# A hybrid diffusion backbone: the first block's modulation quarters between its products, later loads behind its weights, two pieces per mix, GpSimd's low parts in the mLSTM

## The chip, the cores and the metric

One core of a Trainium2 chip runs the whole network in one program. The metric is the time of one execution on the device in microseconds (us); lower is better. Five engines work side by side, each through its own list of instructions: TensorE (PE; its weight loads are shown as PEld), VectorE (DVE), ScalarE (ACT), GpSimd (POOL) and SyncE (SP), which here issues the transfers from memory.

## What is computed

Four layers over 256 context and 256 latent tokens of width 1024, in float32. Each layer has a token mixer (chunked MLP, RG-LRU, mLSTM, chunked MLP) and a convolutional FFN; each is preceded by a norm whose scale and shift come from a projection of the conditioning vectors.

```python
for l in range(DEPTH):
    sh1, sc1, g1, sh2, sc2, g2 = split(silu(c) @ mod_w[l] + mod_b[l])     # latent
    csh1, csc1, cg1, ...       = split(silu(c_ctx) @ mod_w[l] + mod_b[l]) # context
    hl = rms_norm(xl, norm1_g[l]) * (1 + sc1) + sh1                       # hc likewise
    ol, oc = mixer[l % 3](hl, hc)
    xl = xl + g1 * ol
    xl = xl + g2 * conv_ffn(rms_norm(xl, norm2_g[l]) * (1 + sc2) + sh2)
    # context likewise; nothing for it after the last layer
return rms_norm(xl, final_norm_g)

def chunk_mlp(h, w_in, b_in, v_g, v_b, w_s, b_s, w_out):
    u, v = split(gelu(h @ w_in + b_in))            # 2048 each
    v = layer_norm(v, v_g, v_b)
    s = einsum('gpq,bnqgc->bnpgc', w_s, v) + b_s   # mixes the 128 tokens of a chunk
    return (u * s) @ w_out

def mlstm_mixer(h):
    q, k, v, o, g = split(h @ w_in)                # g: input and forget gates
    # cumulative sums of log(sigmoid(forget)), running maxima, decayed scores, both directions
    return (sigmoid(o) * rms_norm(hf + hb) * norm_g) @ w_out
```

## The kernel before, in words

**Layout and products.** Activations lie feature-major: 8 tiles of 128 features (k = 0 to 7), 512 tokens along the free axis, 256 of them context and 256 latent. A weight comes as a tile of 128x1024 floats (0.5 MB) by a transfer of SP (`wsplit`, line 206, three buffers `wr`). It is split into a high part `wh` by ScalarE (L214) and the rest, the low part `wl`, by one subtraction of GpSimd, or of VectorE for every `lo_mix`-th weight (L216 to L218; `lo_mix` is 4 unless set, four buffers for each part). Activations are split alike. A product is three matmuls on the parts (`mm3`: L223 high by high, L224, L225).

**Modulation.** The weights `mod_w` of the scale and shift projections are worked off in pieces: a load of 0.5 MB into one of three buffers `mw` (`mod_load`, L113), then four matmuls with the conditioning vectors (`mod_mul`, L124; the trace shows eight rows for each piece). After eight pieces the sum is copied to `mrow` (L131), turned into columns by two matmuls (L140), and VectorE adds bias and gain (L153, L156). The pieces fill TensorE's list between other work: `pump(n)` adds a credit of n and takes a piece for each whole one. The tuple `PR` (L46) holds the credits by place; its second number is the credit per mix of the first chunk MLP, 1.7. `need` does what is still missing before a norm. There are 176 pieces in all; loads run up to three ahead.

**First block** (`first`, from L1045). The first layer's scale and shift are needed at once, so they come from a copy of their weights in four quarters (`mod_w0`), each giving the columns of two k. The squares of x are summed and the inverse root means brought to PSUM as rows over all partitions (`rp`), then copied to two tiles `rb` by ScalarE. A quarter is four loads (L1070), eight `mod_mul`, `mod_columns`, then `scale_shift` for two k and two streams (L374: nt = x * scale * rb on VectorE; L375: the high part of h on ScalarE; L376: its low part on VectorE), then the products of the first 512 value columns for these two k, and from the second quarter on those of two u tiles.

**Rest of the first chunk MLP.** Three more groups of 512 value columns (each with a load `bv`, L570, used at L575), the products `spatial` of the mixing weights (L602), 16 u tiles, and with a lag of four the 16 mixes (`mix`: L641 mixes the tokens, VectorE and GpSimd multiply and split, then `pump`). The output projection (`out_proj`, weights wo) follows. The FFN begins with a load `cv` (L440).

**mLSTM.** Projection to k by weights that stay (`project_by_stream`), gates from the product with `m_wg`, scans over the tokens on VectorE (`fc` and `mx`, L825 to L828), the rest of k and q, gm's exponential on ScalarE (L849), then the values in two halves (`values`). The readout has a norm and a gate.

**What sets the order.** On SP the order in the first block is that in which the code is written (a manual schedule); elsewhere, and on the other engines throughout, a scheduler sets each engine's list at build time from modelled times. `after(later, earlier)` adds a rule that one instruction is issued after another.

## Time and profile before

| | |
|---|---|
| median of 3 runs | 2141.99 us (2139.78 to 2145.58) |
| the profiled execution | 2143.22 us, its span 2141.1 us |
| granted TensorE clock, mean | 0.975 of full speed |
| transfers | 327.70 MB, mean 153 GB/s |
| PE's share of the chain of waits that ended last | 84% |

The profile comes from one execution. Its span runs from the first to the last instruction; the execution's own time is 2.1 us longer. The page gives each engine's busy time, then the span in 40 slices of 53.5 us. The trace gives each instruction, with what ended the idle time before it on its engine, and busy times and the granted clock for any stretch. Times in the trace are counted from the span's start.

### The profile page before, as it was taken

How to read it: one execution, taken by the hardware profiler on the slowest of the kernel's cores; microseconds unless marked ns; L12 is line 12 of the kernel's file. 1: busy time of each engine (PE TensorE's matmuls, PEld its weight loads, DVE VectorE, ACT ScalarE, POOL GpSimd, SP SyncE). 2: the span in 40 equal slices, each digit the busy share in tenths (PEclk: the TensorE clock that was granted, in tenths of full speed). 3: DMA queues.
4: the chain of work that ended last, by engine and by line, in shares of the span. 5: the costliest groups of instructions: out<-in, count | busy, mean ns of one | idle time of the engine just before them, and what ended most of it. 6: DMA issues, size and time to landing. Idle time of an engine off the chain costs nothing.

```text
span 2141.1 us, 33300 instructions
## 1 busy us (share of the span) xinstructions
PE 2046.9 (96%) x12828; PEld 1746.2 (82%) x12828; DVE 1317.3 (62%) x2816; ACT 895.9 (42%) x1388; POOL 978.3 (46%) x599
## 2 busy tenths in 40 slices
PE   6999999999999999999999999999989999999997
PEld 4787688877778876778777778877889987998997
DVE  4344314766565488957665663626768875847886
ACT  3333222433333146724333332536455555555553
POOL 1334331554444010344444442234358874775784
PEclk9999999999999999989999999999989999998998
DMA  8435533345555435432545453334245655554562
GB/s 333 170 106 186 194 103 114 99 163 171 179 168 169 154 120 187 145 96 63 193 163 187 165 183 94 102 118 151 86 132 184 187 175 165 167 168 131 177 185 90
DMA packets 95425, 327.70 MB, mean 153 GB/s; under 512 B 10529, under 2 KB 12193, under 8 KB 95265
## 3 DMA queue, kind: packets, MB, share of 16 engines
q1 hardware_dynamic: 95264, 325.56, 46.4%
q8 instruction: 101, 1.65, 0.3%
q14 instruction: 60, 0.48, 0.1%
HBM read 324.47 MB, written 1.05 MB: 152 GB/s over the span
## 4 chain that ended last, share of the span: by engine, by line
PE 84%; DVE 8%; ACT 2%; issue 2%; DMA 2%; POOL 1%; SPq 0%; DVEq 0%; ACTq 0%; POOLq 0%
PE ps L223 22%; PE ps L224 21%; PE ps L225 21%; PE ps L124 4%; PE ps L505 3%; PE ps L507 3%; PE ps L506 3%; POOL wl L218 1%; DVE wl L218 1%; PE ps L641 1%; PE ps L932 1%; PE ps L362 1%; DVE nt L374 1%; ACT wh L214 1%; DVE cvo L490 1%
## 5 line engine op out<-in xcount | busy, mean ns | idle before, releaser
L218 POOL TENSOR_TENSOR wl<-wr,wh 128x1024 fp32r<-128x1024 f32 (+2 forms) x329 | 751.8, 2289 | 722.8 <-ACT wh L214 672.6
L214 ACT ACTIVATE wh<-wr 128x1024 fp32r<-128x1024 f32 (+2 forms) x413 | 415.0, 1008 | 741.1 <-PE ps L224 338.2
L490 DVE SCALAR_TENSOR_TENSOR cvo<-ps,cv,cvo 128x189 f32<-128x189 f32 (+2 forms) x1344 | 528.6, 427 | 58.1 <-ACT cvo L479 35.5
L223 PE MATMUL ps<-h,wh 128*128 128x512 f32 (+1 forms) x1256 | 445.0, 365 | 7.4 <-ACT h L375 5.9
L224 PE MATMUL ps<-h,wh 128*128 128x512 f32 (+1 forms) x1256 | 447.9, 359 | 1.8 <-DVE h L376 1.8
L225 PE MATMUL ps<-h,wl 128*128 128x512 f32 (+1 forms) x1256 | 447.2, 359 | 0.0
L223 PEld LDWEIGHTS ps<-h,wh 128*128 128x128 f32 x1256 | 232.3, 189 | 63.6 <-ACT wh L214 9.4
L224 PEld LDWEIGHTS ps<-h,wh 128*128 128x128 f32 x1256 | 238.2, 190 | 36.6 <-DVE h L376 2.6
L225 PEld LDWEIGHTS ps<-h,wl 128*128 128x128 f32 x1256 | 238.1, 190 | 35.7 <-issue 0.2
L218 DVE TENSOR_TENSOR wl<-wr,wh 128x1024 fp32r<-128x1024 f32 (+1 forms) x108 | 138.6, 1284 | 121.8 <-ACT wh L214 120.7
L224 PE MATMUL ps<-hn,wh 128*128 128x256 f32 x608 | 175.5, 289 | 7.0 <-DVE hn L376 6.9
L223 PE MATMUL ps<-hn,wh 128*128 128x256 f32 x608 | 174.9, 288 | 5.8 <-ACT zs L469 3.8
L225 PE MATMUL ps<-hn,wl 128*128 128x256 f32 x608 | 174.7, 288 | 0.0
L505 PE MATMUL ps<-hid,wh 128*128 128x256 f32 (+1 forms) x504 | 156.7, 324 | 8.4 <-ACT hid L234 8.4
L506 PE MATMUL ps<-hid,wh 128*128 128x256 f32 (+1 forms) x504 | 160.2, 322 | 0.9 <-POOL hid L235 0.9
L507 PE MATMUL ps<-hid,wl 128*128 128x256 f32 (+1 forms) x504 | 155.4, 321 | 0.6 <-POOL wl L218 0.6
L481 DVE SCALAR_TENSOR_TENSOR cvo<-ps,cv,cvo 128x255 f32<-128x255 f32 x84 | 40.5, 482 | 169.2 <-ACT cvo L479 169.2
L223 PE MATMUL ps<-prod,wh 128*128 128x256 f32 (+1 forms) x432 | 139.5, 328 | 4.2 <-DVE prod L232 3.1
L224 PE MATMUL ps<-prod,wh 128*128 128x256 f32 (+1 forms) x432 | 139.8, 325 | 1.5 <-POOL prod L235 1.3
L225 PE MATMUL ps<-prod,wl 128*128 128x256 f32 (+1 forms) x432 | 139.6, 325 | 0.6 <-DVE wl L218 0.6
L224 PEld LDWEIGHTS ps<-hn,wh 128*128 128x128 f32 x608 | 119.1, 196 | 8.6 <-DVE hn L376 8.6
L223 PEld LDWEIGHTS ps<-hn,wh 128*128 128x128 f32 x608 | 119.4, 197 | 6.8 <-ACT zs L469 4.6
(241 smaller groups left out, 3579.1 us busy)
## 6 DMA issues: line engine op xcount, KB each, us to landing
mw<-mod_w SPq DMA_DIRECT2D x192, 512.0 KB, 4.7
wr<-w_up SPq DMA_DIRECT2D x168, 512.0 KB, 3.6
wr<-w_dn SPq DMA_DIRECT2D x42, 512.0 KB, 3.7
wr<-cm_wv SPq DMA_DIRECT2D x32, 512.0 KB, 4.1
wr<-cm_wu SPq DMA_DIRECT2D x32, 512.0 KB, 3.6
wr<-cm_wo SPq DMA_DIRECT2D x32, 512.0 KB, 3.7
wr<-w_dn SPq DMA_DIRECT2D x42, 256.0 KB, 2.7
wr<-w_down SPq DMA_DIRECT2D x24, 448.0 KB, 3.4
```

Of the source, the lines that this page charges most:

```text
L124: PE.matmul(mps[0][32 * q:32 * q + 32, :w], ccp[:, k], raw[:, q * w:(q + 1) * w], start=k == 0, stop=k == KT - 1, tile_position=(0, 32 * q ...
L214: S.activation(hi[:, :n], raw[:, :n], AF.Copy)
L218: e.tensor_tensor(lo[:, :n], raw[:, :n], hi[:, :n].bitcast(F32), op=OP.subtract)
L223: PE.matmul(out, lh, rh, start=start, stop=False)
L224: PE.matmul(out, lh, rl, start=False, stop=False)
L225: PE.matmul(out, ll, rh, start=False, stop=stop)
L362: PE.matmul(o, q[:, t * P:(t + 1) * P], ones[:, :1], start=i == t == 0 and q is parts[s][0], stop=q is parts[s][-1], skip_group_check=True)
L481: V.scalar_tensor_tensor(o[:, 1:T], z[:, 0:T - 1], w(3), o[:, 1:T], op0=OP.mult, op1=OP.add)
L490: V.scalar_tensor_tensor(od, zl[:, r0 + dr:r1 + dr, c0 + dc:c1 + dc], w(tap), od, op0=OP.mult, op1=OP.add)
L505: PE.matmul(o, hi[:, sl], rh, start=first, stop=False, skip_group_check=True)
L506: PE.matmul(o, hi[:, sl], rl, start=False, stop=False, skip_group_check=True)
L507: PE.matmul(o, lo[:, sl], rh, start=False, stop=i == FT - 1, skip_group_check=True)
```

## The change

Four things, in the order of the diff:

1. The credit per mix of the first chunk MLP is 2 instead of 1.7.
2. While the first block is written, loads of `mod_w`, of the later `bv` and of `cv` get a rule that they are issued after the block's last weight load (`last_w`).
3. `first` is rearranged. The weights of quarter q+1 (modulation and values) are loaded ahead; quarter q+1's modulation products are written between the value products of k = 2q and those of k = 2q+1, its columns and norm behind the latter. All low parts of weights in the block are VectorE's (`lo_mix` 1). The rows `rp` are read from PSUM by L374, with no copies to `rb`. The `fence` set there is gone.
4. In the mLSTM, after the first products of k, all low parts are GpSimd's (`lo_mix` of a million), until the first half of the values is done.

```diff
@@ -43,7 +43,7 @@
 
 MV = ((1, 0), (2, 4), (3, 5))
 
-PR = (2, 1.7, 0, 2.2, 0, 1.3, 0, 2.2, 0, 2.7, 0, 0, 0)
+PR = (2, 2, 0, 2.2, 0, 1.3, 0, 2.2, 0, 2.7, 0, 0, 0)
 
 KO = (2, 8, 3)
 NHP = 700
@@ -110,10 +110,12 @@
 
     def mod_load(grp, k):
         raw = mwp.tile([P, D], F32, tag="mw", name="mw")
-        SP.dma_start(raw, a["mod_w"][grp[0] * 6 + grp[1] * 2 + grp[2] - 2, k])
+        d = SP.dma_start(raw, a["mod_w"][grp[0] * 6 + grp[1] * 2 + grp[2] - 2, k])
+        if last_w[0] is not None:
+            after(d, last_w[0])
         return raw
 
-    mps = [None]
+    mps, last_w, wdma = [None], [None], [None]
 
     def mod_mul(raw, grp, k):
 
@@ -203,7 +205,7 @@
     lo_mix = [4]
     def wsplit(src, n):
         raw = wraw.tile([P, D], F32, tag="wr", name="wr")
-        SP.dma_start(raw[:, :n], src)
+        wdma[0] = SP.dma_start(raw[:, :n], src)
         return split(raw, n)
 
     def split(raw, n):
@@ -437,7 +439,7 @@
     def ffn(l, streams, npump):
         W = T * len(streams)
         cv = tmp.tile([P, 420], F32, tag="cv", name="cv", bufs=1)
-        SP.dma_start(cv, a["conv"][l])
+        after(SP.dma_start(cv, a["conv"][l]), last_w[0])
         names = [(0, 0), (1, 0), (0, 1), (1, 1)][:STG[3] if len(streams) == 2 else 4]
         Z = {}
         late = ahead[0] is not None
@@ -567,7 +569,9 @@
 
         def evacuate(c, pss):
             bv = tmp.tile([P, 512], F32, tag="cvo", name="bv", bufs=4)
-            SP.dma_start(bv, bass.AP(tensor=a["cm_bv"].tensor, offset=a["cm_bv"][j, c].offset, ap=[[0, P], [1, 512]]))
+            d = SP.dma_start(bv, bass.AP(tensor=a["cm_bv"].tensor, offset=a["cm_bv"][j, c].offset, ap=[[0, P], [1, 512]]))
+            if l == 0:
+                after(d, last_w[0])
             for t in range(ntt):
                 if t % 2 == 0:
                     v[t // 2, c] = big([P, 2, 512], F32, "v")
@@ -796,6 +800,7 @@
         normed(l, 1, [CTX, LAT], h)
         hl = [t[:, :, T:W] for t in h]
         zk = project_by_stream([a["m_wk"][n] for n in range(STG[5])], KT, h, [CTX, LAT], k_outer=True)
+        lo_mix[0] = 10 ** 6
 
         NR = 36
         p = psum()
@@ -974,6 +979,7 @@
                 split_act(prod[i], t, e)
 
         values(0)
+        lo_mix[0] = 4
         gcol = big([P, 4, NR], F32, "gcol")
         pt = psum()
         for t in range(4):
@@ -1052,9 +1058,7 @@
         rsqrt(r, rp[:, :4], 4, 1.0 / D)
         for t in range(4):
             PE.matmul(rp[:, t * P:(t + 1) * P], r[:, t:t + 1].to_broadcast([P, P]), ident, start=True, stop=True)
-        rb = [tmp.tile([P, T], F32, tag=f"acc{s}", name="rb", bufs=1) for s in BOTH]
-        for s in BOTH:
-            S.activation(rb[s], rp[:, s * T:s * T + T], AF.Copy)
+        lo_mix[0] = 1
         pss = [psum() for t in range(4)]
         pu = [psum() for _ in range(2)]
         wu = []
@@ -1063,29 +1067,54 @@
             for k in range(k0, k1):
                 sl = slice(k * P, (k + 1) * P)
                 mm3(pu[n], (wu[n][0][:, sl], wu[n][1][:, sl]), pair(h[k], 0, 2 * T), k == 0, k == KT - 1)
-        for q in range(4):
+        def weights(q):
             grp = (0, 0, q // 2, q % 2)
+            raws = []
             for k in range(0, KT, 2):
                 raw = big([P, 2, 512], F32, "mw0")
                 SP.dma_start(raw.rearrange("p k x -> p (k x)"), a["mod_w0"][q, k // 2])
-                for kk in range(2):
-                    mod_mul(raw[:, kk], grp, k + kk)
+                raws.append(raw)
+            return raws
+
+        def quarter(q, raws):
+            for k in range(KT):
+                mod_mul(raws[k // 2][:, k % 2], (0, 0, q // 2, q % 2), k)
+
+        def norm(q):
             mod_columns(*pend.pop(0))
-            w = wsplit(a["cm_wv"][0, 0, :, q * 1024:q * 1024 + 1024], 1024)
+            for k in (2 * q, 2 * q + 1):
+                for s in BOTH:
+                    scale_shift(0, 1, s, k, rp[:, s * T:s * T + T], h[k][:, :, s * T:s * T + T], [])
+
+        def values(k, w):
+            sl = slice(k % 2 * 512, k % 2 * 512 + 512)
+            for t in range(4):
+                mm3(pss[t], pair(h[k], t * P, t * P + P), (w[0][:, sl], w[1][:, sl]), k == 0, k == KT - 1)
+        def values_w(q):
+            return wsplit(a["cm_wv"][0, 0, :, q * 1024:q * 1024 + 1024], 1024)
+        raws = weights(0)
+        w = values_w(0)
+        quarter(0, raws)
+        norm(0)
+        for q in range(4):
+            if q < 3:
+                nw = values_w(q + 1)
+                nxt = weights(q + 1)
             if q in (1, 2):
                 wu.append(wsplit(a["cm_wu"][0, q - 1], D))
-            for k in (2 * q, 2 * q + 1):
-                norm = []
-                for s in BOTH:
-                    scale_shift(0, 1, s, k, rb[s], h[k][:, :, s * T:s * T + T], norm)
-                sl = slice(k % 2 * 512, k % 2 * 512 + 512)
-                for t in range(4):
-                    mm3(pss[t], pair(h[k], t * P, t * P + P), (w[0][:, sl], w[1][:, sl]), k == 0, k == KT - 1)
+            values(2 * q, w)
+            if q < 3:
+                quarter(q + 1, nxt)
+            values(2 * q + 1, w)
+            if q < 3:
+                norm(q + 1)
             if q > 0:
                 u_tile(0, 0 if q == 1 else 2 * q, 2 * q + 2)
             if q > 1:
                 u_tile(1, 0 if q == 2 else 2 * q, 2 * q + 2)
-        fence[0] = norm[-1]
+            w = nw
+        lo_mix[0] = 4
+        last_w[0] = wdma[0]
         ms.__exit__(None, None, None)
         evacuate(0, pss)
         for i in range(2):
```

The orders below are those of the built programs; line numbers of the change are two to five higher.

VectorE, first block, first two quarters (m: scale and shift columns; nt: x scaled; h: low half of the normed tile; wl: a weight's low part; rb, ps: the root means, in SBUF and in PSUM). Before:

```order
L153 TENSOR_TENSOR m_222<-ps,pc 128x2x2
L156 SCALAR_TENSOR_TENSOR m_219<-m_219,pc 128x2x2
L374 SCALAR_TENSOR_TENSOR nt<-x_82,m_219,rb 128x256 x2
L374 SCALAR_TENSOR_TENSOR nt<-x_83,m_219,rb 128x256 x2
L376 SCALAR_TENSOR_TENSOR h<-nt,m_222,h 128x256 x4
L218 TENSOR_TENSOR wl<-wr,wh 128x1024
```

And with the change:

```order
L220 TENSOR_TENSOR wl<-wr,wh 128x1024
L155 TENSOR_TENSOR m_221<-ps,pc 128x2x2
L155 TENSOR_TENSOR m_224<-ps,pc 128x2x2
L158 SCALAR_TENSOR_TENSOR m_221<-m_221,pc 128x2x2
L376 SCALAR_TENSOR_TENSOR nt<-x_82,m_221,ps 128x256 x2
L376 SCALAR_TENSOR_TENSOR nt<-x_83,m_221,ps 128x256 x2
L378 SCALAR_TENSOR_TENSOR h<-nt,m_224,h 128x256 x4
L220 TENSOR_TENSOR wl<-wr,wh 128x1024
```

The low parts that GpSimd made beside these now stand on VectorE between the norms: two ahead of the first, one behind each of the first two, one inside the third, one ahead of the fourth. On TensorE the second quarter's modulation products stand behind the value products of both first k, not between them; the third's and fourth's stand among the products of the quarter before. On SP two value weights follow the first quarter's four loads, then come the second quarter, a value weight, the third quarter, a u and a value weight, the fourth quarter and the last u weight. Behind these stand the loads that came ahead of the second quarter before: three of `mod_w`, four `bv`, one `cv`.

TensorE, end of the mixes (L641, with the change L645: mixing products; L124, L126: modulation pieces of four; L140, L142: columns; L223 to L227: the products of the output projection). Before:

```order
L124 MATMUL ps<-mw,ccp 32x256 x8
L641 MATMUL ps<-ws,v 128x128 x4
L124 MATMUL ps<-mw,ccp 32x256 x4
L641 MATMUL ps<-ws,v 128x128 x8
L124 MATMUL ps<-mw,ccp 32x256 x12
L140 MATMUL ps<-sel_96,mrow 128x8 x2
L124 MATMUL ps<-mw,ccp 32x256 x4
L641 MATMUL ps<-ws,v 128x128 x4
```

And with the change:

```order
L126 MATMUL ps<-mw,ccp 32x256 x8
L645 MATMUL ps<-ws,v 128x128 x4
L126 MATMUL ps<-mw,ccp 32x256 x4
L645 MATMUL ps<-ws,v 128x128 x5
L142 MATMUL ps<-sel_96,mrow 128x8 x2
L645 MATMUL ps<-ws,v 128x128 x6
L126 MATMUL ps<-mw,ccp 32x256 x4
L645 MATMUL ps<-ws,v 128x128
L225 MATMUL ps<-prod,wh 128x512
```

Of the pieces behind the last projection four now stand among the mixing products, and six follow among the first fifty products of the output projection (behind 5, 20, 24, 26, 45 and 47 of them).

ScalarE, the mLSTM's gates (wh: high part of a weight; km, qm: k and q; gm: the gates). Before:

```order
L841 ACTIVATE km<-ps 128x512 x4
L847 ACTIVATE qm<-ps 128x256
L214 ACTIVATE wh<-wr 128x1024
L847 ACTIVATE qm<-ps 128x256
L849 ACT_TABLE_LOAD
L849 ACTIVATE gm<-gm 36x256
```

And with the change:

```order
L846 ACTIVATE km<-ps 128x512 x4
L852 ACTIVATE qm<-ps 128x256
L854 ACT_TABLE_LOAD
L854 ACTIVATE gm<-gm 36x256
L216 ACTIVATE wh<-wr 128x1024
L852 ACTIVATE qm<-ps 128x256
```

One high part has moved from before gm's exponential to behind it. On VectorE the low part between the scans of mx and the rest of the gates is gone.

## Rows read from the trace of the kernel before

**Rows 1.** The page: busy time by engine, then tenths in 40 slices.

```profile
PE 2046.9 (96%) x12828; PEld 1746.2 (82%) x12828; DVE 1317.3 (62%) x2816; ACT 895.9 (42%) x1388; POOL 978.3 (46%) x599
...
PE   6999999999999999999999999999989999999997
...
PEclk9999999999999999989999999999989999998998
```

**Rows 2.** Timeline, first block: start, length (us), instructions [idle before, releaser].

```profile
29.12 1.95 PE L124 MATMUL ps<-mw,ccp 128*32 128x128 f32 x64
...
32.35 5.89 DVE L374 SCALAR_TENSOR_TENSOR nt<-x,m,rb 128x256 f32<-128x256 f32 x4
...
32.50 5.06 POOL L218 TENSOR_TENSOR wl<-wr,wh 128x1024 fp32r<-128x1024 f32 x2 [12.53 <-ACT wh L214]
...
33.42 0.50 PE L223 MATMUL ps<-h,wh 128*128 128x512 f32 x1 [1.50 <-ACT wh L214]
...
38.69 1.22 PE L225 MATMUL ps<-wh,h 128*128 128x512 f32 x2 [0.25 <-DVE h L376]
...
50.57 1.67 DVE L374 SCALAR_TENSOR_TENSOR nt<-x,m,rb 128x256 f32<-128x256 f32 x4
...
58.38 0.39 PE L223 MATMUL ps<-wh,h 128*128 128x512 f32 x1
...
59.06 0.39 PE L223 MATMUL ps<-wh,h 128*128 128x512 f32 x1
...
77.82 1.98 PE L602 MATMUL ps<-ws,ones 128*128 128x512 f32 x4
```

**Rows 3.** Timeline, end of the mixes, SP's queue and TensorE.

```profile
246.48 0.80 SPq L113 DMA_DIRECT2D mw<-mod_w  x2
...
248.57 18.62 SPq L113 DMA_DIRECT2D mw<-mod_w  x7
...
251.33 0.64 PE L124 MATMUL ps<-mw,ccp 128*32 128x256 f32 x8 [0.27 <-DMA mw<-mod_w]
...
255.94 1.08 PE L124 MATMUL ps<-mw,ccp 128*32 128x256 f32 x8 [3.98 <-DMA mw<-mod_w]
```

**Rows 4.** Windows there: stretch, length, busy PE PEld DVE ACT POOL, PEclk, DMA, GB/s.

```profile
250.00:254.00 4.00, 1.70 (x21) 0.61 (x19) 3.57 (x5) 1.59 (x3) 2.66 (x3) 1.00 0.91 295
254.00:264.00 10.00, 7.49 (x35) 5.20 (x36) 1.68 (x4) 1.28 (x3) 2.00 (x3) 0.50 0.62 220
```

**Rows 5.** Timeline, the mLSTM's gates.

```profile
1383.61 2.41 POOL L218 TENSOR_TENSOR wl<-wr,wh 128x1024 fp32r<-128x1024 f32 x1 [2.43 <-ACT wh L214]
...
1383.98 3.11 DVE L825 TENSOR_TENSOR_SCAN fc<-lf,t 4x512 f32<-4x512 f32 x1
...
1391.54 1.21 DVE L825 TENSOR_TENSOR_SCAN mx<-t,ig 4x512 f32<-4x512 f32 x1
...
1394.26 1.22 DVE L218 TENSOR_TENSOR wl<-wr,wh 128x1024 fp32r<-128x1024 f32 x1
...
1395.53 0.80 PE L224 MATMUL ps<-wl,h 128*128 128x512 f32 x1 [5.50 <-DVE wl L218]
```

**Rows 6.** Windows there, columns as in rows 4.

```profile
1390.00:1395.50 5.50, 0.03 (x1) 0.00 (x0) 5.35 (x7) 0.00 (x0) 0.44 (x2) 0.87 0.00 0
1395.50:1401.00 5.50, 5.47 (x13) 4.32 (x14) 2.88 (x14) 1.86 (x4) 3.51 (x1) 0.51 0.59 192
```

**Rows 7.** Windows of the first 40 us, columns as in rows 4.

```profile
0.00:20.00 20.00, 7.52 (x81) 6.50 (x81) 7.43 (x23) 8.31 (x14) 2.79 (x6) 1.00 0.92 342
20.00:40.00 20.00, 14.95 (x104) 11.04 (x105) 11.63 (x23) 6.90 (x13) 5.06 (x2) 0.80 1.02 399
```

**Rows 8.** Timeline, TensorE: norm of first FFN, of second FFN, mLSTM readout.

```profile
354.55 1.50 PE L124 MATMUL ps<-mw,ccp 128*32 128x256 f32 x24
...
961.55 1.01 PE L223 MATMUL ps<-h,wh 128*128 128x256 f32 x3 [1.19 <-ACT h L375]
...
1522.44 1.06 PE L124 MATMUL ps<-mw,ccp 128*32 128x256 f32 x14
```

## The prediction

> **What bounds the kernel now.** I read the page first: TensorE is busy for 2046.9 of 2141.1 us, and of 40 slices only the first and the last are well below nine tenths; the clock falls below nine tenths in four [rows 1]. What is lost inside the others, windows of a few us show. Work on the other engines costs nothing unless TensorE waits for it. So the change is worth what it takes from TensorE's waits and from the stretches in which its granted clock is at the lower level (1.2 of 2.4 GHz), and that is settled place by place. I went on to the timeline of the first 80 us, of the end of the first mixer's mixes, and of the mLSTM's gates.
>
> First block, second quarter [rows 2]: its modulation products begin at 29.12 and take 1.95, and TensorE goes on with the next tiles at 33.42. Then the four nt take 5.89 us, because two low parts of GpSimd run in the same stretch; the first low half of h reaches TensorE at 38.69. The row of 50.57 is to be read beside that of 32.35: the same four instructions, 1.67 us with GpSimd idle.
>
> End of the mixes [rows 3]: after the last projection the pieces of modulation follow each other faster than their weights land, and one waits 3.98 us. The stretches show the whole price [rows 4]: TensorE idles 4.0 - 1.70 = 2.3 and 10.0 - 7.49 = 2.5 us, and 7.49 busy us at a granted clock of 0.50 lose another 3.7: 8.5.
>
> mLSTM's gates [rows 5, 6]: the second product of the values waits 5.50 us for a low part that stands on VectorE behind the gate scans. Idle 5.5; then 5.47 busy us at 0.51 lose 2.7. Together 8.2.
>
> **The change part by part**, against the profiled execution (2143.2 us; the runs' median is 2142.0, 1.2 below).
>
> *First block.* All six low parts go to VectorE; the later loads (three of mod_w, four bv, cv: 2.8 MB) no longer stand on SP ahead of the second quarter; rb is read from PSUM, which I cost at nothing (bounds 0 and 0.4 for four nt: the rows of nt differ by that much only beside GpSimd). Up to 33.42 I leave the instants as they are: the new order still has quarter 1 behind the products of both first tiles, and its columns with nothing beside them. From there TensorE has 120 products of 512 columns; three take 59.06 - 58.38 = 0.68 [rows 2], so 27.2 us; two quarters of 1.95, 3.9; four pieces (8 rows each; 24 rows are 1.50, so 0.5 each [rows 8]), 2.0; some five gaps of 0.3 where it changes to modulation products, 1.5. The third norm has a low part of VectorE (1.22 [rows 5]) behind its columns and loses some 1.0 to it; the later columns have 12 and 18 products of u beside them, 2.7 and 4.1 us. The sum is 33.4 + 35.6 = 69.0 for the spatial products, which now begin at 77.82. Three pieces fewer are done by then, 1.5: 77.8 - 69.0 - 1.5 = 7.3; I take **7.0** (bounds 3, as in rival 2, and 9, with no wait left). Are the weights there? At 342 and then 399 GB/s [rows 7] 6.8 MB are in at 20 us and 14.8 at 40; the last quarter ends with the 13.4th, in at 37, wanted near 52. On ScalarE quarter 0's mrow now stands behind a second wh, whose weight ends with the 5.5th MB, in at 16 to 17: nothing, at most 1 us.
>
> *More pieces per mix* (1.7 to 2): always two. A piece costs 0.5 wherever TensorE has other work, and the number of all pieces stays. After the last projection there are ten instead of nine, but the order now has four of them among the mixes and six among the first 50 products of the output projection. Measured from the end of the last projection, loads are issued at +1.7 (two, [rows 3]: 246.48) and the second is used at 251.33, 4.9 us on; the next ones land about 1.6 us apart (0.5 MB at the 295 GB/s of [rows 4]). By that the fourth piece, at +7, has its weight at +6; the fifth, at +8.4, at +6.6; the sixth, at +12.4, at +11 (its own, 248.57 to 255.94, is 7.4 at most). None waits: gain **8.5** (bounds 0 and 8.5).
>
> *mLSTM.* The low parts of wk, wq and the values' first weights go to GpSimd. That of the values' first, at 1394.26 on VectorE, follows the one of 1383.61 on GpSimd: 1383.61 + 2 x 2.41 = 1388.4, or 1389.6 if a scan of 1.21 gets in between; TensorE comes there by 1390.0: no wait. But the scheduler moved the next wh behind gm's exponential on ScalarE, and gm waits for the scans. A scan that met GpSimd took 3.11, one without 1.21 [rows 5]. With the first scan let in at 1386.0, the second behind the next low part, to 1390.3, and five more of 0.7 to 1.2, gm is ready near 1395.0, the wh at 1396.5, and its low part, 2.41, at 1399.0. TensorE's other 23 products end at 1390.0 + 5.2 = 1395.2; it waits 1.3 and, one product later, 2.3. Waits of this length are followed by the lower clock in [rows 4, 6], so its 2.7 is charged as before: 6.3 instead of 8.2, gain **1.9** (bounds -1 and 8.2).
>
> The Trainium skill, SBUF — State Buffer, Who interferes with whom, states that a VectorE instruction with two SBUF inputs and a GpSimd instruction that reads SBUF exclude each other for a whole instruction. The trace agrees at both places (5.89 against 1.67, 3.11 against 1.21), so the rule speaks for the first block's part and against this one. Were the scans not held up, gm would be ready at 1390.6 and the low part at 1394.6, and the gain here would be the whole 8.2.
>
> *What the pieces leave.* Five pieces ahead all along, fillers stand elsewhere. The 24 rows of 1.50 us in the norm of the first ffn are gone; 2.75 pieces now stand in the norm of the second, where TensorE waits 1.19 [rows 8]. I let the two change places: 0 (bounds -5 and +5, a wait of 1.3 with the 3.7 of half speed). In the readout the 14 rows of 1.06 us at 1522.44, ahead of a broadcast that waits for VectorE, are missing: **-1.1** (bounds -5 and 0). The mLSTM's norm gets two pieces; 0 to 1.0, taken as 0. SP issues no transfer more, and cv, bv and mod_w, now later, are wanted tens of us after they land.
>
> Sum: 7.0 + 8.5 + 1.9 - 1.1 = 16.3; 2143.2 - 16.3 = **2127**.
>
> **Rivals.**
> (1) The end of the mixes still waits: ten pieces, three buffers, and the products that should fill need wo's weights from the same SP queue. For: loads of a burst land 1.6 us apart. Against: in the new order seven of wo stand ahead of the burst. That part gains 0: 2135.5.
> (2) VectorE becomes the first block's bound, three of its low parts late by 1.22 ahead of a norm: 2127 + 3.7 = 2131. Against: their weights land 5 us or more before, by the rates above.
> (3) The gates' wait goes altogether, the scans getting in between: 2127 - 6.3 = 2121.
> (4) Slower: the fillers spent early leave five gaps bare (norms of the first ffn and the LRU, three of the readout), and the clock falls in each. One costs its 1.5 us and, as at 254 to 264, 3.7 of half speed: 5.2; five are 26, 2153. From four on (20.8) it outweighs the 16.3; beyond 0.3% it takes all five. Against: from 31.07 to 33.42 TensorE had nothing but the columns, and its next product took 0.50, where two at the lower clock take 1.22 [rows 2].
> (5) The change doesn't do what its words say: quarter 1 is not between its block's products in the order. That is in the sum already; the first block's gain comes from GpSimd's absence, and 2127 stands.
>
> **How the numbers follow.** A measurement of this kernel tells about 0.3% (6.4 us) from no change; the lines are 2135.6 and 2148.4. Chances: forecast, with (5), 0.62; (1) 0.11; (2) 0.09; (3) 0.09; (4) 0.03; 0.06 for stretches such as the LRU's, reordered either way by a few us. Faster takes the forecast, (2), (3), half of (1) and most of the rest: 0.88; within 0.3% 0.09; slower 0.03. The range reaches from 2117 ((3) with the first block's upper bound, less the 1.2 of the median) to 2138 ((1) with half the readout's lower bound).
>
> **What would show it.** Right: in the first block's second norm four nt below 0.5 us each and no GpSimd row beside them; the spatial products near 69 us; no wait for mod_w over 1 us near 240 us, and the upper clock level there; at the gates no wait for VectorE's low part, but one of some 3.6 us behind gm's exponential. Wrong: waits for wl in the first block, a wait for mod_w among the output products, or as many half-speed stretches as now.

## The result, and the profile after

The change takes 2118.35 us (median of 4 runs, 2116.24 to 2122.96) against 2142.93 of the kernel before (4 runs): a ratio of 0.9894 (95% interval 0.9882 to 0.9906). The profiled execution took 2119.53, its span 2117.8, that is 23.3 less than before. The page, its parts 1 and 2, against [rows 1]:

```profile
PE 2038.5 (96%) x12828; PEld 1739.3 (82%) x12828; DVE 1314.6 (62%) x2819; ACT 895.6 (42%) x1386; POOL 970.2 (46%) x596
...
PE   6999999999999999999999999999889999998997
...
PEclk9999999999999999999999999999989999998998
```

The same 12828 products of TensorE (matmuls, as the trace counts them) are busy for 8.4 us less (more of them at the upper level of the clock), and the idle time fell from 94.2 to 79.3 us, by 14.9. Together 23.3. Where it fell, the view of waits says: what TensorE waited for, total us, times, longest. Before:

```profile
PE ps L124 <- DMA mw<-mod_w: 5.8, 3, 4.0
PE ps L224 <- DVE wl L218: 5.5, 1, 5.5
...
PE ps L966 <- DVE rs L287: 2.0, 2, 1.3
```

After (L226 is L224, L971 is L966; no wait for `mod_w` is left in the view):

```profile
PE ps L971 <- DVE rs L289: 4.2, 2, 2.2
...
PE ps L226 <- POOL wl L220: 0.3, 1, 0.3
```

To place all of the 23.3 us, I took the time of each product of TensorE in both traces, leaving out the modulation pieces, and from the lead of the change half a us for each piece that it had done more (or less) by then [rows 8]. The lead grows or shrinks so:

| place (us in the trace of before) | forecast | measured |
|---|---|---|
| first block (to 100) | 7.0 | 6.9 |
| end of the mixes (240 to 300) | 8.5 | 7.8 |
| norm of the first FFN (345 to 365) | 0 | -2.2 |
| from there to the end of the RG-LRU (940) | 0 | 1.9 |
| norm of the second FFN (960) | 0 | 3.4 |
| from there to the gates (1380) | 0 | 0.8 |
| mLSTM's gates (1380 to 1400) | 1.9 | 7.6 |
| values, readout and next projection (to 1600) | -1.1 | -2.9 |
| the rest | 0 | 0.0 |

Not every row belongs to the change alone. The same measure on the repetition of the change (the last run below) gives 7.4 for the first block, 7.7 for the end of the mixes and 7.7 for the gates, but 1.9 instead of 3.4 in the norm of the second FFN, +1.3 instead of -2.9 from the values to 1600, and -2.2 for the rest.

First block, timeline, against [rows 2]:

```profile
29.52 1.95 PE L126 MATMUL ps<-mw,ccp 128*32 128x128 f32 x64
...
32.75 1.66 DVE L376 SCALAR_TENSOR_TENSOR nt<-x,m,ps 128x256 f32<-128x256 f32 x4
...
33.83 0.50 PE L225 MATMUL ps<-wh,h 128*128 128x512 f32 x1 [1.51 <-ACT h L377]
...
45.08 0.50 PE L225 MATMUL ps<-wh,h 128*128 128x512 f32 x1 [0.35 <-ACT h L377]
...
69.47 1.98 PE L606 MATMUL ps<-ws,ones 128*128 128x512 f32 x4
```

The four nt of the second norm take 1.66 us where they took 5.89, and the spatial products begin at 69.47; 69.0 was forecast. Two things differ for these nt: no low part of GpSimd runs beside them, and they read the root means from PSUM (`ps`) instead of SBUF (`rb`). The trace of the kernel before tells the second apart: in later norms 13 nt with `ps` run beside a low part of GpSimd, and each takes 0.47 or 0.48 us, as without one, where an nt with `rb` took up to 2.59. Two of them, begun 0.1 us after the low part, with the low half of h behind them (timeline, before):

```profile
1346.11 1.89 POOL L218 TENSOR_TENSOR wl<-wr,wh 128x800 fp32r<-128x800 f32 x1 [7.64 <-PE ps L367]
1346.21 0.87 DVE L374 SCALAR_TENSOR_TENSOR nt<-x,m,ps 128x256 f32<-128x256 f32 x2
...
1347.26 1.01 DVE L376 SCALAR_TENSOR_TENSOR h<-nt,m,h 128x256 fp32r<-128x256 f32 x1 [0.18 <-ACT h L375]
```

So the read from PSUM alone would have made nt short; the low half of h (1.01 here, 0.47 alone) still loses to GpSimd.

End of the mixes, windows, against [rows 4] (stretch, length, busy us and instructions of PE PEld DVE ACT POOL, granted clock, DMA share, GB/s):

```profile
242.00:246.00 4.00, 4.00 (x38) 3.47 (x38) 3.66 (x7) 1.00 (x2) 1.27 (x1) 1.00 0.83 270
246.00:256.00 10.00, 10.00 (x70) 6.00 (x72) 4.25 (x8) 3.56 (x5) 5.42 (x5) 1.00 0.74 247
```

TensorE does not idle there at all, and the clock stays at the upper level: 70 rows in ten us where there were 35.

The gates, timeline, against [rows 5]:

```profile
1366.47 3.12 DVE L830 TENSOR_TENSOR_SCAN fc<-lf,t 4x512 f32<-4x512 f32 x1
...
1377.24 0.42 ACT L854 ACTIVATE gm<-gm 36x256 f32<-36x256 f32 x1 [5.72 <-DVE gm L839]
...
1378.69 4.86 POOL L220 TENSOR_TENSOR wl<-wr,wh 128x1024 fp32r<-128x1024 f32 x2 [6.70 <-ACT wh L216]
...
1381.24 0.50 PE L226 MATMUL ps<-wl,h 128*128 128x512 f32 x1 [0.33 <-POOL wl L220]
```

The wait of 5.50 us is gone, and so is the one of 3.6 in all that was forecast in its place: 0.33 is left. It is 0.32 in the repetition and 0.44 in the run with the later loads not held back, but 1.40 to 1.52 in five other runs below whose code at the gates is the same. In those five, GpSimd's low part behind gm's exponential takes 3.6 us; in the first three it takes 2.5, and one of VectorE's small casts beside it 2.42 instead of 0.21. Some 1.1 of the 7.6 us come and go with that.

The readout: two waits for the broadcast, which pieces had shortened before, now 4.2 us instead of 2.0.

```profile
1498.02 0.71 PE L971 MATMUL ps<-ident,rs 128*128 128x128 f32 x4 [2.21 <-DVE rs L289]
...
1508.61 1.22 PE L971 MATMUL ps<-ident,rs 128*128 128x128 f32 x4 [2.03 <-DVE rs L289]
```

### The profile page after: what moved, and what is told of

It reads as the page before. It is cut to its first block, busy times and chain, and to the rows that moved or that the text cites. A ratio compares the mean times of both kernels' runs of the same rounds, so it can differ in the third digit from the quotient of the medians.

```text
span 2117.8 us, 33271 instructions
## 1 busy us (share of the span) xinstructions
PE 2038.5 (96%) x12828; PEld 1739.3 (82%) x12828; DVE 1314.6 (62%) x2819; ACT 895.6 (42%) x1386; POOL 970.2 (46%) x596
## 3 DMA queue, kind: packets, MB, share of 16 engines
q8 instruction: 101, 1.65, 0.3%
## 4 chain that ended last, share of the span: by engine, by line
PE 87%; DVE 6%; ACT 3%; issue 2%; POOL 1%; DMA 1%; SPq 0%; DVEq 0%; ACTq 0%; POOLq 0%
PE ps L225 23%; PE ps L226 22%; PE ps L227 22%; PE ps L126 4%; PE ps L507 4%; PE ps L509 4%; PE ps L508 3%; POOL wl L220 1%; PE ps L645 1%; PE ps L364 1%; DVE wl L220 1%; ACT wh L216 1%; DVE cvo L492 1%; PE ps L937 1%; DVE nt L376 0%
## 5 line engine op out<-in xcount | busy, mean ns | idle before, releaser
L220 POOL TENSOR_TENSOR wl<-wr,wh 128x1024 fp32r<-128x1024 f32 (+1 forms) x326 | 742.7, 2283 | 719.4 <-ACT wh L216 624.4
L226 PE MATMUL ps<-h,wh 128*128 128x512 f32 (+1 forms) x1256 | 448.5, 360 | 1.5 <-DVE h L378 1.5
L227 PE MATMUL ps<-h,wl 128*128 128x512 f32 (+1 forms) x1256 | 447.5, 359 | 0.0
L226 PEld LDWEIGHTS ps<-h,wh 128*128 128x128 f32 x1256 | 238.5, 190 | 35.5 <-DVE h L378 1.9
L227 PEld LDWEIGHTS ps<-h,wl 128*128 128x128 f32 x1256 | 238.3, 190 | 35.5
L226 PE MATMUL ps<-hn,wh 128*128 128x256 f32 x608 | 175.7, 289 | 10.0 <-DVE hn L378 9.9
L227 PE MATMUL ps<-hn,wl 128*128 128x256 f32 x608 | 174.8, 288 | 0.0
L226 PE MATMUL ps<-prod,wh 128*128 128x256 f32 (+1 forms) x432 | 139.7, 325 | 2.9 <-POOL prod L237 2.7
L227 PE MATMUL ps<-prod,wl 128*128 128x256 f32 (+1 forms) x432 | 138.8, 324 | 0.6 <-DVE wl L220 0.6
L226 PEld LDWEIGHTS ps<-hn,wh 128*128 128x128 f32 x608 | 119.0, 196 | 11.8 <-DVE hn L378 11.8
```

The source lines that it names most:

```text
L220: e.tensor_tensor(lo[:, :n], raw[:, :n], hi[:, :n].bitcast(F32), op=OP.subtract)
L226: PE.matmul(out, lh, rl, start=False, stop=False)
L227: PE.matmul(out, ll, rh, start=False, stop=stop)
```

## The experiments

Each kernel ran beside runs of the kernel before; ratios are to those. Where a stage is spoken of, its times come from the profile of the run, against that of the change.

### The first block: GpSimd, the order, the loads

**GpSimd's low parts back in the first block**

```diff
-        lo_mix[0] = 1
+        lo_mix[0] = 4
         pss = [psum() for t in range(4)]
```

> The change, but in the first block GpSimd makes the low parts again (every fourth is VectorE's). Theory: two things give the first block's gain, the absence of GpSimd beside the norms and the modulation products that now stand beside the columns. Without the first, the four nt of a norm that meets a low part take near 6 us instead of 1.7, TensorE waits over 1 us in that norm and the lower clock returns for some us: the spatial products begin at 73 to 75 instead of 69.5, the whole is 4 to 5 us longer. Rival: the order of the transfers and of the products makes the gain alone; then the spatial products stay at 69.5 to 70.5.

Measured: 0.9911 (0.9893 to 0.9929). The spatial products begin at 75.56, 6.1 us later than in the change. It was the first norm that GpSimd met here, not the second (timeline):

```profile
18.05 4.65 POOL L220 TENSOR_TENSOR wl<-wr,wh 128x1024 fp32r<-128x1024 f32 x2 [16.98 <-ACT wh L216]
...
20.98 1.74 DVE L158 SCALAR_TENSOR_TENSOR m<-m,pc 128x4 f32<-128x4 f32 x1
...
23.83 0.79 PE L225 MATMUL ps<-wh,h 128*128 128x512 f32 x1 [3.09 <-ACT h L377]
```

One tiny instruction on 4 columns, 0.16 us in the change, takes 1.74 beside GpSimd's low part; TensorE waits 3.09 instead of 1.51. The Trainium skill (SBUF — State Buffer, Who interferes with whom) says that it is issue order, not the shape of an operation, that decides who blocks; the row agrees: 128x4 lost 1.6 us to a 128x1024 that had begun first. Against the expectation no nt was long: in all four norms the four together took 1.65 or 1.66. In the third norm GpSimd slowed the four low halves of h, which read SBUF alone:

```profile
49.43 5.95 DVE L378 SCALAR_TENSOR_TENSOR h<-nt,m,h 128x256 fp32r<-128x256 f32 x4
```

In the whole the run's interval overlaps that of the change.

**Quarters behind all products of the quarter before**

```diff
             values(2 * q, w)
-            if q < 3:
-                quarter(q + 1, nxt)
             values(2 * q + 1, w)
-            if q < 3:
-                norm(q + 1)
...
                 u_tile(1, 0 if q == 2 else 2 * q, 2 * q + 2)
+            if q < 3:
+                quarter(q + 1, nxt)
+                norm(q + 1)
             w = nw
```

> The change, but a quarter's modulation products, columns and norm are written behind all products of the quarter before, so that the columns stand bare again. All low parts of the block stay VectorE's, the loads stay as they are. Theory: the third and the fourth norm each bring back a wait of about 2.0 us (0.5 for mrow, 1.5 for the first high half of h) where the change has 0.35 in all: the spatial products begin at 72.5 to 73.5. If they begin at 69.5 to 70, what is gained comes from GpSimd's absence alone, as the prediction had it in its fifth rival.

Measured: 0.9897 (0.9878 to 0.9915), no difference from the change in the whole; but the spatial products begin at 74.68, 5.2 later (4.2 without the two pieces that then stand ahead of them). The third norm (timeline):

```profile
45.28 0.39 PE L142 MATMUL ps<-sel,mrow 128*128 128x8 f32 x2 [0.46 <-ACT mrow L133]
...
47.18 0.79 PE L225 MATMUL ps<-wh,h 128*128 128x512 f32 x1 [1.51 <-ACT h L377]
```

The order is worth about as much as GpSimd's absence. With either one missing, 4 to 6 us of the block's 6.9 are lost. By the measure of the table 3.6 us are still lost ahead of the gates; most of the loss goes between 1500 and 1600, where the change's own profile has stretches at a lower clock (last section), so the whole does not show it.

**The later loads not held back**

```diff
-        if last_w[0] is not None:
-            after(d, last_w[0])
...
-        after(SP.dma_start(cv, a["conv"][l]), last_w[0])
+        SP.dma_start(cv, a["conv"][l])
...
-            if l == 0:
-                after(d, last_w[0])
```

> The change, but the later loads (three of mod_w, four bv, one cv, 2.8 MB) are not held back: they stand on SP ahead of the second quarter's weights again. Theory: the weights of the second quarter land 7 us later, at 30 instead of 23, and TensorE wants them at 29.5; the later ones land 2 us or more ahead of their use. The spatial products begin 0.5 to 1.5 us later than the 69.5 of the change. Rival: the held loads are the point of the rearranged block; then the block is 5 us or more later.

Measured: 0.9898 (0.9878 to 0.9918); the spatial products at 71.13, 1.7 later. The second quarter's modulation waits for its weights (timeline):

```profile
30.58 0.65 PE L124 MATMUL ps<-mw,ccp 128*32 128x128 f32 x16 [0.64 <-DMA mw<-mod_w]
```

Only this 0.64 has a cause that the trace shows. Seven other runs have the first block just as it is in the change: in six the spatial products begin at 68.9 to 69.4, in one at 71.5, with a granted clock of 0.66 instead of 0.83 from 20 to 30 us. So holding the loads back is at most a small part.

### The credit per mix

**1.7 again**

```diff
-PR = (2, 2, 0, 2.2, 0, 1.3, 0, 2.2, 0, 2.7, 0, 0, 0)
+PR = (2, 1.7, 0, 2.2, 0, 1.3, 0, 2.2, 0, 2.7, 0, 0, 0)
```

> The change with the credit per mix at 1.7 again. Theory: the waits for mod_w behind the last projection come back with their clock (2.3 + 2.5 + 3.7 = 8.5 us there), and so do the fillers that the change had spent: three pieces in the norm of the first FFN (2 us), five in the readout of the mLSTM (3 to 4 us). So the credit is worth much less than 8.5 in the whole: this kernel 3 to 6 us slower than the change, 2121 to 2125. Rival: the fillers cost nothing where they are missing; then it is 8 us slower, 2127.

Measured: 0.9944 (0.9921 to 0.9966), 2129.77: some 11 us slower than the change, against 3 to 6 expected. At the end of the mixes the loss is 8.1, in the norm of the first FFN 2.2 come back, in the readout some 3, all near what was expected. What was not expected: 3.1 us in the norm of the RG-LRU, where pieces that the norm needs wait for their weights, and 4.8 at the gates, where no low part of VectorE stands (timelines):

```profile
737.26 0.62 PE L126 MATMUL ps<-mw,ccp 128*32 128x256 f32 x2 [2.04 <-DMA mw<-mod_w]
...
1390.98 0.80 PE L226 MATMUL ps<-wl,h 128*128 128x512 f32 x1 [3.16 <-POOL wl L220]
```

So the expectation fell: this credit also reaches places a thousand us later. The next part follows the second of them.

### The gates

**Both lines in the mLSTM undone**

```diff
-        lo_mix[0] = 10 ** 6
...
         values(0)
-        lo_mix[0] = 4
```

> The change without its two lines in the mLSTM: low parts of the q and value weights again on VectorE at every fourth. Theory: the wait of 5.5 us at the gates and the lower clock behind it come back, 8 us and no more, 2126. Rival (the prediction's own term): the change has only traded one wait for another there, and the whole gets 2 us longer, 2120.

Measured: 0.9913 (0.9888 to 0.9937), 2125.28, by the ratios 4 us above the change; at the gates 4.9 us are lost, neither 8 nor 2: the wait for VectorE's low part is 3.64, not the 5.50 of before.

**Only the low part of the first q weight on VectorE**

```diff
+            lo_mix[0] = 1 if n == 0 else 10 ** 6
             z = project(a["m_wq"][n], KT, hl, T)
```

> The change, but the low part of the first q weight alone is VectorE's. No instruction of TensorE waits for it. Theory: it takes near 2.6 us beside GpSimd's and ends after the low part that would have freed a buffer first; the next two q weights are then loaded together, the first of them lands near 5.4 instead of 3.5 us behind its issue, its high part holds up ScalarE ahead of the gates' exponentials, and the gates' scans begin about 2.9 us later (measured from the stage's start). The second value weight's high part stands behind gm's exponential, so TensorE waits about 3 us for its low part and runs at the lower level of the clock for some us: 4 to 6 us longer, 2122 to 2124. Rival: only a low part that TensorE waits for counts; then nothing changes, 2118.

Measured: 0.9887 (0.9868 to 0.9906). In the whole it can't be told from the change, but at the gates 3.7 us are lost (2.56 of wait), by a low part for which TensorE does not wait. The theory is right in kind. Some 1.1 of the 3.7 are not this low part's, though: GpSimd's low part behind gm's exponential took 3.58 here, as in the five runs named above. Nor is the theory right in size: the loads of the next q weights, issued 1.1 us later (measured from the stage's start), landed within 3.6 and 4.5 us, not 5.4, and the scans began 1.2 us later, not 2.9.

**Only the low part of the first value weight on VectorE**

```diff
+                if c == 0:
+                    lo_mix[0] = 1 if q == 0 else 10 ** 6
                 hi, lo = wsplit(a["m_wv"][c, :, q * 1024:(q + 1) * 1024], 1024)
```

> The change, but the low part of the first value weight alone is VectorE's, behind the gates' scans. Theory: the scans begin as in the change, so the low part comes 2.9 us earlier than before, and TensorE waits 2.4 to 3 us for it instead of 5.5, with some us at the lower level behind it: 3 to 5 us longer than the change, 2121 to 2123. Together with the run for the first q weight this should make up the 8 us of the run with both. Rival: the wait is 5.5 as before, and this part alone is worth the 8 us.

Measured: 0.9895 (0.9877 to 0.9913); TensorE waits 2.48, as expected, and 2.1 us are lost at the gates; the whole can't be told from the change. With the 3.7 of the run before that is 5.8, not the 8 that both were to make. What ended the waits in these three runs, in their order (timelines):

```profile
1379.88 0.50 PE L226 MATMUL ps<-wl,h 128*128 128x512 f32 x1 [3.64 <-DVE wl L220]
```

```profile
1384.73 0.79 PE L226 MATMUL ps<-wl,h 128*128 128x512 f32 x1 [2.56 <-POOL wl L220]
```

```profile
1381.06 0.50 PE L226 MATMUL ps<-wl,h 128*128 128x512 f32 x1 [2.48 <-DVE wl L220]
```

Undoing the two lines alone thus loses 4.9 of the 7.6 us at the gates. The missing 2 to 3 us are in the transfers; the two parts overlap, since the credit of 1.7 alone loses 4.8 there. In the two kernels with the credit of 1.7 (before, and the run above) the third q weight lands late. Transfers of 7 us around its issue and landing, first the kernel before, then the run with 1.7, then the change (queue: packets, MB, share of 16 engines; then issues, KB, median us to landing):

```profile
q8 instruction: 1, 0.02, 1.8%
...
wr<-m_wq SPq DMA_DIRECT2D x2, 512.0 KB, 5.8
```

```profile
q8 instruction: 1, 0.02, 2.4%
...
wr<-m_wq SPq DMA_DIRECT2D x2, 512.0 KB, 5.4
```

```profile
q1 hardware_dynamic: 325, 1.20, 55.8%
...
wr<-m_wq SPq DMA_DIRECT2D x2, 512.0 KB, 3.6
```

In the first two a transfer of the instruction queue, 16 KB, stands beside the loads; 2.4% of 16 engines over 7 us are 2.7 us of one of them. The page counts 101 such transfers before as after, one for some 254 of TensorE's 25656 rows (12828 products and as many weight loads). Where they fall depends on how many rows TensorE has done, pieces included. That can be moved.

**TensorE's list moved by 34 products, in the change**

```diff
     V.memset(ones, 1.0)
+    dz = psum()
+    for _ in range(34):
+        PE.matmul(dz[:, :1], ones, ones[:, :1], start=True, stop=True)
```

> The change, with 34 products of one column into a PSUM tile that nobody reads, at the start, where TensorE has nothing to do before 12 us. Each is four rows of TensorE in the trace, so all later transfers of TensorE's code (16 KB, one for every 256 rows or so) come half a page earlier in its list: the one at 1368.4 near the gates then comes near 1357.6, beside the load of the third q weight (issued at 1356.5 in the change, landed 3.5 us later). Theory: a code transfer that meets this load makes it land about 2 us later; the gates' scans begin that much later, and TensorE waits 1.5 to 2.5 us for the low part of the second value weight instead of 0.33. Rival: loads of that stretch land late for another reason (the order on SP, which is the same here); then the wait stays below 0.6 us. The whole time may go either way by a few us, since the other code transfers move too.

Measured: 0.9925 (0.991 to 0.994). Inconclusive as a test. The added products are not free: they keep TensorE until 15.7 us, the sums of squares that began at 12.13 in the change stand behind them, and the spatial products begin at 74.42, 5.0 later, which is most of the 7.5 us that the whole loses (timeline):

```profile
1.05 14.67 PE L90 MATMUL ps<-ones 128*128 128x1 f32 x68 [1.05 <-DVE ones L87]
```

At the gates the transfer came beside the load, but only 0.5 us behind its issue, and was short, 0.9% of 16 engines over 7 us, or 1.0 us; the load was not late.

```profile
q8 instruction: 1, 0.02, 0.9%
...
wr<-m_wq SPq DMA_DIRECT2D x2, 512.0 KB, 3.7
```

TensorE's wait did grow, to 1.52, but not by the scans, which began as in the change. Here GpSimd's low part behind gm's exponential took 3.60, as in the four runs that have the same gates, no such products and waits of 1.40 to 1.48; so the growth is not the shift's. Timeline of this run:

```profile
1385.86 3.60 POOL L223 TENSOR_TENSOR wl<-wr,wh 128x1024 fp32r<-128x1024 f32 x1 [6.70 <-ACT wh L219]
...
1389.51 0.50 PE L229 MATMUL ps<-wl,h 128*128 128x512 f32 x1 [1.52 <-POOL wl L223]
```

**The list moved by 32 products, with the credit of 1.7**: the two edits together.

> The run with the credit of 1.7, with 32 such products at the start. There a code transfer at 1363.9 stood beside the load of the third q weight, which landed 5.9 us behind its issue, and TensorE waited 3.16 us at the gates with no low part of VectorE there. Theory: moved by half a page, the transfer misses the load; it lands near 3.6 us behind its issue, the scans begin 2.3 us earlier, and the wait is 0.5 to 1.2 us. Rival: the wait belongs to the credit itself (other fillers ahead of the stage); then it stays near 3.2 us.

Measured: 0.9947 (0.9931 to 0.9964), no faster in the whole than without the shift: the added products cost 3.7 us at the start (spatial products at 72.56 against 68.90). At the gates it is as the theory says: no code transfer in those 7 us, the two q weights land in 3.5 and 3.6 us, and the wait falls from 3.16 to 1.36, the loss there from 4.8 to 1.0 (transfers; timeline):

```profile
q1 hardware_dynamic: 313, 1.15, 59.5%
...
wr<-m_wq SPq DMA_DIRECT2D x2, 512.0 KB, 3.5
```

```profile
1392.55 0.50 PE L229 MATMUL ps<-wl,h 128*128 128x512 f32 x1 [1.36 <-POOL wl L223]
```

Moving the list by half a block removes the late landing, at the same credit. That it is the code transfer that delays the load is the reading that fits these runs, and another load of the kept traces bears it out. The second q weight, issued near 1331 us in the change, has the same loads around it in eight runs with the change's credits and the change itself. In six it landed in 3.4 to 3.9 us, with no code transfer begun beside it; in three, the change among them, in 6.1 to 6.9, with a code transfer of 1.9 to 2.9 us begun 1.1 to 2.4 us behind its issue. The change and its repetition are one program (the load by itself, first the change, then the repetition):

```profile
DMA to landing us min/median/max: 6.1/6.1/6.1
```

```profile
DMA to landing us min/median/max: 3.4/3.4/3.4
```

The same code transfer began at 1331.5 in the one and at 1337.0 in the other, so the number of rows does not place it alone. Most meetings do little. Over all 14 traces, loads of 512 KB with no other load beside them for their first 2.2 us landed in 3.55 us (median) where no code transfer began in the first 3.4 us, and 10 of 1247 took over 4.3; where one did, the median is 3.64, and 25 of 191 took over 4.3. Of the 31 with the transfer begun 0.7 to 2.0 us behind the issue it was 16. What makes such a meeting long stays open.

### Where pieces are worth more

**Five pieces kept for the readout**

```diff
-PR = (2, 2, 0, 2.2, 0, 1.3, 0, 2.2, 0, 2.7, 0, 0, 0)
+PR = (2, 2, 0, 2.2, 0, 1.3, 0, 2, 0, 2.7, 0, 0, 0)
```

> The change with the credit in the second FFN at 2.0 instead of 2.2, so that five pieces are kept for the mLSTM's readout. Theory: the two waits of 2.0 to 2.2 us for the broadcast in the readout, with the lower clock behind them, are filled again: 3 to 4 us faster than the change, 2114 to 2115.5. Rival: the pieces only move a wait; then it stays within 1 us of the change, 2118.

Measured: 0.9871 (0.985 to 0.9893), the lowest ratio of all, though its interval overlaps that of the change. The two waits in the readout fell from 4.24 to 2.33:

```profile
1500.07 0.68 PE L971 MATMUL ps<-ident,rs 128*128 128x128 f32 x4 [1.19 <-DVE rs L289]
...
1510.35 0.80 PE L971 MATMUL ps<-ident,rs 128*128 128x128 f32 x4 [1.14 <-DVE rs L289]
```

Its span, 2117.4, is within 0.4 us of that of the change. The mechanism is seen; that the kernel is faster is not shown.

**Pieces in the RG-LRU's output projection**

```diff
-PR = (2, 2, 0, 2.2, 0, 1.3, 0, 2.2, 0, 2.7, 0, 0, 0)
+PR = (2, 2, 0, 2.2, 0, 1.3, 0.6, 1.8, 0, 2.7, 0, 0, 0)
```

> The change with a credit of 0.6 per product tile of the RG-LRU's output projection, which had none, and 1.8 instead of 2.2 in the second FFN, so that pieces still reach the mLSTM's readout. Theory: the five waits of 0.5 to 1.0 us there (4.0 in all) and the lower clock behind them (6.8 us at half speed, 3.4) are filled, 4 to 6 us less, and the readout keeps its fillers as in the run with 2.0 in the FFN, 3 us less: 2110 to 2113. Rival: pieces among products that wait for VectorE and GpSimd come too late or too early to fill them, or bring waits for mod_w; then it is no faster than the change.

Measured: 0.9897 (0.9881 to 0.9912), no faster; the expectation fell. The waits there stay (0.96, 0.95, 0.71 us are the first three; 0.94, 0.97, 0.72 in the change), and a piece in the norm behind it waits for its weight:

```profile
955.76 1.06 PE L126 MATMUL ps<-mw,ccp 128*32 128x256 f32 x2 [2.23 <-DMA mw<-mod_w]
```

**The change once more**

> The change itself, beside the run before it on the same chip: 2116 to 2121.

Measured: 2118.37, 0.9889 (0.9876 to 0.9903); span 2115.8.

## Why the prediction came out as it did

The time, 2118.35, lies in the range of 2117 to 2138, near its lower end and 8.6 below the point. The direction and the two large terms were right; one term was far too small.

**First block: right, with a wrong reason beside it.** 7.0 forecast, 6.9 measured. Rival (5) said that the gain comes from GpSimd's absence. The run with the quarters apart denies that: it loses 4.2 us with all low parts on VectorE. What filled the third and fourth columns was in the sum (the products of u beside them) but was not named as a part of the gain. Quarter 1's columns stayed bare, as read from the order: 1.51 us. Reading PSUM was put at nothing, and the whole fall of nt from 5.89 to 1.67 was put down to GpSimd. Either of the two alone makes nt short: with `rb` and GpSimd idle four took 1.67 [rows 2], and with the means in PSUM each takes 0.47 or 0.48 beside GpSimd too. The sum is the same, but its reason is only one of two. GpSimd's absence still counts, for the small column instruction and the low halves of h: bringing it back costs 6.1.

**End of the mixes: right.** 8.5 forecast, 7.8 measured, no wait, upper level. The rate by which the weights land was enough, so rival (1) did not come.

**Gates: the step that failed.** The text took gm to be ready near 1395.0, from a first scan at 1383.98 as in the kernel before, and so forecast a new wait of 1.3 and 2.3 us and a gain of 1.9. The chain from the first scan to gm's exponential is as forecast: 11 us, measured 1377.24 - 1366.47 = 10.8. Its start is not: with the lead of 14.6 us at that point it would have been 1369.4, and it was 1366.47, 2.9 earlier. About 1.1 of it is the low part of the first q weight: on VectorE it ended late beside GpSimd's, and the next loads waited for that (shown by the run with that low part alone). The other 1.8 is the landing of the third q weight in 3.5 us instead of 5.4, which goes with the pieces, not with the low parts (alone, in the run with 1.7, the late landing is worth 2.4). The forecast wait itself is real: with the load late and all low parts on GpSimd, the run with 1.7 waits 0.34 and 3.16 us, 3.5 against the 3.6 forecast, some 1.1 of it by a low part of 3.58 us instead of the 2.41 reckoned with. I had looked at each low part for the product that needs it, and not for the buffer that it frees. So rival (3), the whole wait gone, is what happened, though not by its mechanism (scans getting in between GpSimd's low parts): the scan at the start still took 3.12 us. That no more than 0.33 of wait is left was luck besides: five runs with the same gates keep 1.40 to 1.52.

**The SBUF rule.** It was weighed as speaking for the first block and against the gates. It held at the gates, where beside GpSimd the first scan still takes 3.12 us, against 1.21 for the scan without it [rows 5]; it only did not decide the term. In the first block it accounts for the 5.89 of before, where nt read x and `rb`. But the Trainium skill (SBUF — State Buffer, Who interferes with whom) states it for two inputs in SBUF, and the nt of the change have one, x. The trace agrees: with GpSimd back in the first block no nt is long, but h and the small column instruction are. The prediction did not see that the change's own read from PSUM takes nt out of the rule.

**What the pieces leave.** Counted as nothing but 1.1 in the readout. In the profiled execution the norm of the first FFN lost 2.2, that of the second won 3.4, the readout and what follows lost 2.9, the RG-LRU's part won 1.9. They nearly cancel, as the forecast let them, but not for its reason; and of these only the first FFN's and the RG-LRU's are alike in the repetition. Rival (4) had pieces spent early as a cost only; the run with 1.7 shows a gain as well: five pieces ahead, the RG-LRU's norm does not wait for `mod_w`. All in all taking back the credit costs some 11 us, the first block gained 7, taking back the gates' lines costs 5. That these make about the 23.3 is partly chance: the first and the last of them share some 2 us at the gates, and single places scatter by up to 3.

## What to carry to other kernels

Follow a moved operation to its buffer: ask which load waits for the buffer that it frees, and what stands behind that load, before pricing the wait at the product. Where an instruction is slow beside another engine, look at where each of its operands lies as well as at the other engine: here one operand in PSUM instead of SBUF was enough for nt. Fillers that are spent early are missing later, but they also turn a forced load into one that has long landed, so try the number of fillers as a whole and look at every norm. A difference of some us at one place of one profile is not yet the place's own: run the same kernel twice first.

## What the runs showed of the hardware

**Transfers of code beside loads.** The Trainium skill (Runtime: NRT & Kernel Launch, Instruction fetch mechanics) says that code comes in blocks of 16 KiB, 256 instructions, by a queue of the sequencer's own, and that the cost is mostly hidden. The trace agrees on the blocks (101 transfers, 1.65 MB, for 25656 rows of TensorE) and on TensorE: none of its waits over 0.2 us is put down to one. But the data loads beside two of them landed in 5.4 and 5.8 us (medians of two), where without one they took 3.5 and 3.6, and one load of the change landed in 6.1 that took 3.4 in the repetition. Such losses are rare: of the 191 loads counted above that met a transfer, 25 took over 4.3 us, the longest 5.9. A kernel that adds or moves rows of TensorE moves these meetings.

**The clock is not the same from one execution to the next.** The change and its repetition are one program; from 1538 to 1546 both are busy without a gap (windows, first the change, then the repetition):

```profile
1538.00:1546.00 8.00, 8.00 (x43) 8.00 (x43) 1.63 (x10) 0.00 (x0) 0.00 (x0) 0.57 0.28 94
```

```profile
1538.00:1546.00 8.00, 8.00 (x69) 8.00 (x69) 2.97 (x14) 1.29 (x3) 0.03 (x1) 1.00 0.29 97
```

A granted clock of 0.57 in the one and 1.00 in the other, 43 rows and 69, with waits before them that agree to a few hundredths of a us but for one (the two executions stand 0.2 us apart at 1530). Near 960 and 1900 it is the other way round, by 1.5 and 3.1 us. So single places of two profiles compare to about 1.5 to 3 us, unless a wait shows the cause; that bounds what the table above says of its small rows.
